# GpSimd's share of the weight splitting: four subtractions of 256 columns in place of one of 1024

## The chip, the core and the metric

The kernel runs on one core of a Trainium2 chip. The metric is the device time of one execution in microseconds, as the median of several executions. The core has a matrix engine (TensorE, written PE in the profile, with its weight loads apart as PEld), VectorE (DVE), ScalarE (ACT), GpSimd (POOL) and SyncE (SP), which here only issues loads and stores. Each engine works through its own list of instructions in order, and semaphores tie the lists together.

## The reference

One decoder layer over 512 tokens of width 1024, all in float32: a norm, one wide projection, three token mixers (dilated window attention, a gated recurrence, block attention), their gated sum, an output projection, and a gated feed-forward block, with a last norm. Cut to its frame:

```python
def hybrid_layer(x, ...):
    h = rms_norm(x, g_mix)
    z = h @ w_in                                   # 1024 x 7936
    qa, ka, va, xb, gb, qc, kc, vc, gates = jnp.split(z, offs, axis=-1)
    ...                                            # A: 12 heads in three dilations
    o_b = rg_lru_branch(xb, gb, conv_w, conv_b, ...)
    o_c = moba_attention(qc, kc, vc, rel_bias[:, A_HEADS:])
    gt = jax.nn.sigmoid(gates).reshape(B, S, 3, D)
    merged = gt[:, :, 0] * (o_a @ p_a) + gt[:, :, 1] * (o_b @ p_b) + gt[:, :, 2] * (o_c @ p_c)
    x = x + merged @ w_out
    u = rms_norm(x, g_ffn) @ w_gu
    gate, up = jnp.split(u, 2, axis=-1)
    return x + (jax.nn.silu(gate) * up) @ w_down
```

## The kernel before

**Split products.** The kernel keeps float32 accuracy by writing each operand as a high half (rounded to the type `F32R`) and a low half (what the rounding left out), and by forming three products for each pair: high by high, high by low, low by high (`mm3`, lines 195 to 198). Nearly all of TensorE's work is these triples, with 512 columns each.

**Weight chunks.** All weights are packed on the host into 149 chunks of 128 x 1024 floats, in the order in which the program uses them (`chunk_plan`). `stage_g` (lines 164 to 182) brings in one chunk in three steps: SyncE issues the load into `wraw` (line 177), ScalarE rounds it into the high half `whi` (line 178), and an engine subtracts, `wlo = wraw - whi` (line 179). That engine is GpSimd for the chunks 7 to 61 and VectorE for the others, by this line:

```python
eng = nc.gpsimd if 6 < i < N_POOL else nc.vector     # N_POOL = 62
```

There are 3 buffers of `wraw` and 4 each of `whi` and `wlo`. `chunk` stages up to two chunks ahead of the one that is handed out. Chunks 7 to 61 belong to the projections of the three mixers and of the gates, up to about 410 us of the run.

**Stages.** The order of the program is: norm statistics and the first projections; values for mixer A and its four head groups j (`la`, `wa`, `wa2`, `ta`, `xa`) woven between projections; mixer C head pairs (`lc`, `wc`, `tc_`, `xcm`); mixer B in four blocks (`b_head`, `b_gate`, `b_tail`, `b_end`); the gated merge; the output projection; the feed-forward block (from about 500 us on) and the down projection with the last norm.

**Places that the text below speaks of.** `ea` with `q_tiles` and `k_tiles` makes the operands of the logits from scaled projections `qt` and `kt` (lines 465, 515, 520). `values_out` (lines 450, 451) copies values out of PSUM. `renorm` (line 922) scales the eight reloaded tiles `xt` by the norm. `class_logits` (lines 572 to 585) multiplies and adds biases; its last step (line 581) is what frees its PSUM bank for the next projection. `wa` (line 590: exponentials on ScalarE) stores its sums through a small DRAM tile `exch`, and `wa2` (lines 721 to 741) reads the partner's sums back, makes a factor in a chain of tiny VectorE steps (lines 724, 726, 727, 732, 735, 737, 739, with one exponential on ScalarE, line 729) and scales the probabilities (line 595). `flip` and `flip_pairs` transpose these on TensorE (lines 604 and 618). `b_tail` and `b_end` (lines 887 to 897) end mixer B: `gb = gb * a` on VectorE (line 896), rounded by ScalarE (line 248).

**What sets the order.** The program is written in one order, and a scheduler in the program builder sets the list of each engine from it, by its own estimate of how long each instruction takes (`schedule_with_timeline_sim=True`, line 1334). So an instruction that is cut into pieces can move others. It also tracks which part of a tile an instruction reads or writes.

Of the kernel before, what the change touches and what calls it, by code (L numbers as in the profile page):

```python
# [131 lines left out]
def layer_kernel(tc, x0p, xT, wts, tab, oneh, msk, idn, gfin, out):  # L132
    nc = tc.nc
# [3 lines left out]
    with (  # L137
# [10 lines left out]
        def uid(s):  # L148
            cnt[0] += 1
            return f"{s}_{cnt[0]}"  # L150

        def slot(dt=F32, s="s"):
            return sp.tile([128, 512], dt, name=uid(s), tag="s")
# [4 lines left out]
        def f32(ap):  # L158
            return ap.bitcast(F32)
# [4 lines left out]
        def stage_g():  # L164

            i = pos[0]
            if i >= len(plan):
                return
            pos[0] += 1
            raw = wp.tile([128, 1024], F32, name=uid("wraw"), tag="wraw", bufs=3)  # L170
            hi = wp.tile([128, 1024], F32R, name=uid("whi"), tag="whi", bufs=4)
            lo = wp.tile([128, 1024], F32R, name=uid("wlo"), tag="wlo", bufs=4)
            eng = nc.gpsimd if 6 < i < N_POOL else nc.vector
            n = FIRST_W if i < 2 else 1024
            for c in range(0, 1024, n):
                cc = slice(c, c + n)
                nc.sync.dma_start(raw[:, cc], wts[i, :, cc])
                nc.scalar.copy(hi[:, cc], raw[:, cc])  # L178
                eng.tensor_sub(lo[:, cc], raw[:, cc], f32(hi[:, cc]))  # L179
                if i < 2:  # L180
                    yield
            ready.append((plan[i][0], hi, lo))

        def stage():
            for _ in stage_g():
                pass
# [78 lines left out]
        xts = []  # L265
        X = []
        parts = [stage_g(), stage_g()]
        for k in range(KT):
            if k == 0:
# [4 lines left out]
            for p in FIRST[k]:  # L274
# [3 lines left out]
            hi = slot(F32R, "xhi")  # L278
            nc.scalar.activation(hi, xt, AF.Copy, scale=g)
            lo = slot(F32R, "xlo")  # L280
            nc.vector.scalar_tensor_tensor(
                lo, in0=xt, scalar=g, in1=f32(hi), op0=ALU.mult, op1=ALU.subtract
# [798 lines left out]
        for m in range(8):  # L1081
# [7 lines left out]
            for b in (0, 2, 1):  # L1089
                ps = bank()  # L1090
                nk = len(O[b])
                for k in range(nk):
                    hi, lo = pc[kk // 8]
                    c = slice((kk % 8) * 128, (kk % 8) * 128 + 128)
# [17 lines left out]
        for m in range(8):  # L1112
# [9 lines left out]
            hi = slot(F32R, "uhi")  # L1122
            nc.scalar.activation(hi, x1, AF.Copy, scale=g)
            lo = slot(F32R, "ulo")
# [70 lines left out]
        for tb in range(4):  # L1195
# [4 lines left out]
            for c0, c1 in cuts:  # L1200
                hf, cc = c0 // 512, slice(c0 % 512, c0 % 512 + c1 - c0)
# [15 lines left out]
                eng = nc.vector if c1 == 1024 and tb == 3 else nc.gpsimd  # L1217
# [9 lines left out]
            for c0, c1 in ((0, 256), (256, 512), (512, 1024)) if tb == 3 else ((0, 512), (512, 1024)):  # L1227
                hf, cc = c0 // 512, slice(c0 % 512, c0 % 512 + c1 - c0)
                y = y2[hf][:, cc]
                nc.vector.tensor_scalar(out=y, in0=y, scalar1=r0, scalar2=t3, op0=ALU.mult, op1=ALU.mult)  # L1230
                eng = nc.sync if c0 != 256 else nc.scalar
# [106 lines left out]
```

## Time and profile before

| | |
|---|---|
| median of 3 executions | 902.32 us (902.29 to 904.23) |
| profiled execution: its own time | 902.25 us |
| its span, first to last instruction | 900.5 us |
| mean granted TensorE clock | 0.991 of full speed |
| TensorE busy | 881.0 us (98%) |
| VectorE busy | 489.2 us (54%) |
| ScalarE busy | 398.8 us (44%) |
| GpSimd busy | 249.6 us (28%), of it 135.2 us in the 55 subtractions of line 179 |

Times in the views are microseconds from the span's start; "mean ns" and the min/median/max of one line are nanoseconds. In a timeline each row gives start, duration, engine, line, operation, tile written from tiles read, shape and count, and in brackets how long the engine had idled before and what ended the idle time. A duration runs from the start of the instruction on its engine to its end, so an instruction that was held up after its start shows a long duration and no idle time. PEclk is the granted clock of TensorE: 1.00 is the upper of its two levels (2.4 GHz), 0.50 the lower (1.2 GHz).

### The profile page before, as it was taken

To read this page: it belongs to the slowest core of one execution; us is meant where nothing else is said; L and a number is where in the kernel's file an instruction comes from. 1 tells how busy PE (TensorE), PEld (TensorE's weight loads), DVE (VectorE), ACT (ScalarE), POOL (GpSimd) and SP (SyncE) were. 2 spreads that over 40 slices of the span, in tenths; PEclk is the share of its full clock that TensorE was granted. 3 is DMA by queue.
4 is the path that set the end of the run, shared out by engine and by line. 5 is a ranking of instruction groups with operands and counts; after the bars stand their busy time and mean duration, and the time that the engine had idled before them with its cause. 6 is when DMAs were issued, how large, how long until landed. Compare 5 with 4: busy or idle time off the path is not lost.

```text
span 900.5 us, 11072 instructions
## 1 busy us (share of the span) xinstructions
PE 881.0 (98%) x4166; PEld 739.8 (82%) x4166; DVE 489.2 (54%) x922; ACT 398.8 (44%) x692; POOL 249.6 (28%) x163
## 2 busy tenths in 40 slices
PE   9998999989999999999999999999999999999996
PEld 7887988868888888878888888888888888888885
DVE  7498957575665566765533536444444444322226
ACT  7375754654666556872222434333223322211213
POOL 2144353444343333346311221111111122100004
PEclk9999999999999999999999999999999999999999
DMA  7254332542322221123222413222322222222202
GB/s 277 86 160 98 98 118 71 114 113 80 110 89 82 94 94 71 71 94 117 94 102 86 140 71 108 95 91 88 109 96 94 94 94 93 97 106 103 93 24 94
DMA packets 40278, 90.27 MB, mean 100 GB/s; under 512 B 13988, under 2 KB 15780, under 8 KB 40224
## 3 DMA queue, kind: packets, MB, share of 16 engines
q1 hardware_dynamic: 34048, 88.26, 29.4%
q10 hardware_dynamic: 5824, 0.98, 0.7%
q8 instruction: 33, 0.54, 0.2%
q0 software_dynamic: 352, 0.33, 0.1%
q14 instruction: 21, 0.17, 0.1%
HBM read 87.34 MB, written 2.20 MB: 99 GB/s over the span
## 4 chain that ended last, share of the span: by engine, by line
PE 82%; DVE 10%; ACT 5%; issue 1%; DMA 1%; SPq 0%; DVEq 0%; ACTq 0%
PE ps L196 22%; PE ps L197 22%; PE ps L198 21%; PE ps L1185 12%; PE ps L655 1%; PE ps L604 1%; DVE xt L922 1%; DVE gb L896 1%; PE ps L551 1%; ACT whi L178 1%; PE ps L550 1%; ACT P L590 1%; DVE P L595 1%; DMA xt<-in_xT 1%; DVE a L891 1%
## 5 line engine op out<-in xcount | busy, mean ns | idle before, releaser
L178 ACT CAST whi<-wraw 128x1024 fp32r<-128x1024 f32 (+1 forms) x149 | 154.5, 1038 | 267.4 <-issue 101.7
L196 PE MATMUL ps<-hi,whi 128*128 128x512 f32 x520 | 206.3, 397 | 1.1 <-ACT hi L248 1.1
L197 PE MATMUL ps<-lo,whi 128*128 128x512 f32 x520 | 203.8, 392 | 0.2 <-DVE lo L249 0.2
L198 PE MATMUL ps<-hi,wlo 128*128 128x512 f32 x520 | 203.6, 392 | 0.0
L179 POOL TENSOR_TENSOR wlo<-wraw,whi 128x1024 fp32r<-128x1024 f32 x55 | 135.2, 2460 | 226.4 <-ACT whi L178 226.0
L179 DVE TENSOR_TENSOR wlo<-wraw,whi 128x1024 fp32r<-128x1024 f32 (+1 forms) x94 | 118.2, 1258 | 113.8 <-ACT whi L178 113.8
L196 PE MATMUL ps<-uhi,whi 128*128 128x512 f32 x352 | 137.9, 392 | 0.0
L198 PE MATMUL ps<-uhi,wlo 128*128 128x512 f32 x352 | 137.1, 389 | 0.0
L197 PE MATMUL ps<-ulo,whi 128*128 128x512 f32 x352 | 136.9, 389 | 0.0
L198 PEld LDWEIGHTS ps<-hi,wlo 128*128 128x128 f32 x520 | 98.2, 189 | 20.7
L196 PEld LDWEIGHTS ps<-hi,whi 128*128 128x128 f32 x520 | 98.4, 189 | 20.4 <-ACT hi L248 1.5
L197 PEld LDWEIGHTS ps<-lo,whi 128*128 128x128 f32 x520 | 98.4, 189 | 19.4 <-DVE lo L249 0.5
L1159 POOL TENSOR_TENSOR av<-sg,uu 128x512 f32<-128x512 f32 x22 | 45.8, 2080 | 198.4 <-DVE sg L1157 198.4
L198 PEld LDWEIGHTS ps<-uhi,wlo 128*128 128x128 f32 x352 | 66.1, 188 | 14.0
L196 PEld LDWEIGHTS ps<-uhi,whi 128*128 128x128 f32 x352 | 66.1, 188 | 13.5
L197 PEld LDWEIGHTS ps<-ulo,whi 128*128 128x128 f32 x352 | 66.1, 188 | 13.4
L1185 PE MATMUL ps<-wlo,hi 128*128 128x512 f32 (+1 forms) x180 | 57.7, 384 | 0.0
L1185 PE MATMUL ps<-whi,lo 128*128 128x512 f32 (+1 forms) x180 | 57.6, 384 | 0.0
L1185 PE MATMUL ps<-whi,hi 128*128 128x512 f32 (+1 forms) x180 | 57.2, 384 | 0.0
L1155 DVE TENSOR_TENSOR uu<-ps,rb 128x512 f32<-128x512 f32 x22 | 15.2, 690 | 64.9 <-PE ps L198 64.9
L196 PE MATMUL ps<-whi,xhi 128*128 128x256 f32 (+1 forms) x128 | 40.7, 322 | 0.3 <-DVE stn L558 0.3
L197 PE MATMUL ps<-wlo,xhi 128*128 128x256 f32 (+1 forms) x128 | 40.9, 319 | 0.0
(232 smaller groups left out, 1223.1 us busy)
## 6 DMA issues: line engine op xcount, KB each, us to landing
wraw<-in_wts SPq DMA_DIRECT2D x145, 512.0 KB, 3.2
xt<-in_xT SPq DMA_DIRECT2D x15, 256.0 KB, 5.5
bias<-relb SPq DMA_DIRECT2D x8, 256.0 KB, 5.9
xr<-in_xT SPq DMA_DIRECT2D x8, 256.0 KB, 2.7
out<-y SPq DMA_DIRECT2D x7, 256.0 KB, 2.1
wraw<-in_wts SPq DMA_DIRECT2D x4, 256.0 KB, 4.8
bias<-relb SPq DMA_DIRECT2D x4, 128.0 KB, 3.8
bias<-relb SPq DMA_DIRECT2D x8, 64.0 KB, 3.9
```

What stands on the lines that cost most here:

```text
L178: nc.scalar.copy(hi[:, cc], raw[:, cc])
L179: eng.tensor_sub(lo[:, cc], raw[:, cc], f32(hi[:, cc]))
L196: nc.tensor.matmul(o, lh, rh, start=start, stop=False)
L197: nc.tensor.matmul(o, lh, rl, start=False, stop=False)
L198: nc.tensor.matmul(o, ll, rh, start=False, stop=stop)
L550: nc.tensor.matmul(bk, qh[:, qc], kk[:, k0 : k0 + nn], start=True, stop=False)
L551: nc.tensor.matmul(bk, ql[:, qc], kk[:, k0 : k0 + nn], start=False, stop=True)
L590: nc.scalar.activation(lay[qb][0], lay[qb][0], AF.Exp, scale=-1.0, bias=negm[:, qb : qb + 1], accum_out=den[:, qb : qb + 1])
L595: nc.vector.tensor_scalar(out=lay[qb][0], in0=lay[qb][0], scalar1=f[:, qb : qb + 1], scalar2=None, op0=ALU.mult)
L1155: nc.vector.tensor_mul(uu, pu, r2)
L1159: nc.gpsimd.tensor_mul(av, sg, uu)
L1185: nc.tensor.matmul((acc[tb][hf] if o is None else o)[:, cc], l[:, t], r[:, hf * 512 + cc.start : hf * 512 + cc.stop], start=((k == 0 or fi ...
```

## The change

Where GpSimd does the subtraction, the chunk's 1024 columns are subtracted in four instructions of 256 columns. VectorE's chunks keep one instruction. Nothing else in the source changes, and the arithmetic is the same.

```diff
                 nc.scalar.copy(hi[:, cc], raw[:, cc])
-                eng.tensor_sub(lo[:, cc], raw[:, cc], f32(hi[:, cc]))
+
+                p = 256 if eng is nc.gpsimd else n
+                for d in range(c, c + n, p):
+                    dd = slice(d, d + p)
+                    eng.tensor_sub(lo[:, dd], raw[:, dd], f32(hi[:, dd]))
```

In the changed file every line behind this one stands four lines further on: its line 590 of before is 594, and so on. The numbers in the tile names (`whi_2079`) also shift.

In GpSimd's list each chunk's subtraction becomes a run of four. Before, around the chunks that are used near 100 us:

```order
L179 TENSOR_TENSOR wlo_975<-wraw_973,whi_974 128x1024
L179 TENSOR_TENSOR wlo_981<-wraw_979,whi_980 128x1024
L179 TENSOR_TENSOR wlo_1163<-wraw_1161,whi_1162 128x1024
L179 TENSOR_TENSOR wlo_1169<-wraw_1167,whi_1168 128x1024
L610 MEMSET ph_1226 128x128
```

After:

```order
L183 TENSOR_TENSOR wlo_996<-wraw_994,whi_995 128x256 x4
L183 TENSOR_TENSOR wlo_1005<-wraw_1003,whi_1004 128x256 x4
L183 TENSOR_TENSOR wlo_1190<-wraw_1188,whi_1189 128x256 x4
L183 TENSOR_TENSOR wlo_1199<-wraw_1197,whi_1198 128x256 x4
L614 MEMSET ph_1259 128x128
```

The order of the chunks among GpSimd's other work stays as it was.

ScalarE's list changes where the last head group of mixer A takes its exponentials (`P` and `dd` are the probabilities and their sums, `z` a gate, `ee` the factor of `wa2`), at 186 to 191 us of the profile. Before:

```order
L590 ACTIVATE P_1943,dd_2030<-P_1943,stp_1868 128x128
L590 ACTIVATE P_1964,dd_2030<-P_1964,stp_1868 128x128
L178 CAST whi_2079<-wraw_2078 128x1024
L905 ACTIVATE z_1903<-ps_1910 128x512
L590 ACTIVATE P_1943,dd_2030<-P_1943,stp_1868 128x128
L590 ACTIVATE P_1964,dd_2030<-P_1964,stp_1868 128x128
L590 ACTIVATE P_1943,dd_2030<-P_1943,stp_1868 128x128
L590 ACTIVATE P_1964,dd_2030<-P_1964,stp_1868 128x128
L729 ACTIVATE ee_1989<-df_1986 128x8
```

After:

```order
L178 CAST whi_2145<-wraw_2144 128x1024
L909 ACTIVATE z_1963<-ps_1973 128x512
L594 ACTIVATE P_2006,dd_2093<-P_2006,stp_1925 128x128
L594 ACTIVATE P_2027,dd_2093<-P_2027,stp_1925 128x128
L594 ACTIVATE P_2006,dd_2093<-P_2006,stp_1925 128x128
L594 ACTIVATE P_2027,dd_2093<-P_2027,stp_1925 128x128
L594 ACTIVATE P_2006,dd_2093<-P_2006,stp_1925 128x128
L594 ACTIVATE P_2027,dd_2093<-P_2027,stp_1925 128x128
L733 ACTIVATE ee_2052<-df_2049 128x8
```

The rounding of a chunk and a gate's activation, which stood in the middle of the eight exponentials, now stand ahead of them.

On TensorE the rows that move near there are these (lines 604 and 618 are transposes of the scaled probabilities, 196 to 198 a gate's projection). Before, at 193 to 199 us:

```order
L604 MATMUL ps_2106<-ident,P_1704 128x128 x3
L196 MATMUL ps_2084<-hi_966,whi_1905 128x512
L197 MATMUL ps_2084<-lo_967,whi_1905 128x512
L198 MATMUL ps_2084<-hi_966,wlo_1906 128x512
L618 MATMUL ps_2119<-ident,P_1727 128x128 x4
L618 MATMUL ps_2136<-ident,P_1748 128x128
L196 MATMUL ps_2157<-hi_931,whi_2046 128x512
L197 MATMUL ps_2157<-lo_932,whi_2046 128x512
L618 MATMUL ps_2136<-ident,P_1748 128x128 x3
L198 MATMUL ps_2157<-hi_931,wlo_2047 128x512
```

After:

```order
L200 MATMUL ps_2153<-hi_987,whi_1965 128x512
L608 MATMUL ps_2160<-ident,P_1757 128x128 x2
L608 MATMUL ps_2160<-ident,P_1758 128x128
L608 MATMUL ps_2175<-ident,P_1758 128x128 x3
L201 MATMUL ps_2153<-lo_988,whi_1965 128x512
L202 MATMUL ps_2153<-hi_987,wlo_1966 128x512
L622 MATMUL ps_2188<-ident,P_1781 128x128 x4
L622 MATMUL ps_2205<-ident,P_1802 128x128
L200 MATMUL ps_2229<-hi_952,whi_2109 128x512
L201 MATMUL ps_2229<-lo_953,whi_2109 128x512
L202 MATMUL ps_2229<-hi_952,wlo_2110 128x512
L622 MATMUL ps_2205<-ident,P_1802 128x128 x3
```

One matmul moves ahead of the transposes of line 604, and one ahead of the last three of line 618; the rest keeps its place. Up to 178 us TensorE's list differs only inside the projection of the values at 50 to 57 us, and VectorE's list up to 220 us not at all. SyncE issues one bias load behind the eight reloads of `xt` (58 us) that it issued ahead of them.

## The prediction

> **What bounds the kernel now.** I read the page's engine shares first, then the busy time by stage, then what TensorE waits for, then the timeline at each wait.
>
> ```profile
> PE 881.0 (98%) x4166; PEld 739.8 (82%) x4166; DVE 489.2 (54%) x922; ACT 398.8 (44%) x692; POOL 249.6 (28%) x163
> ```
>
> TensorE is the bound, so only its idle time and its slow time can be won. By stage (columns: length, PE busy, then the other engines, granted clock, DMA):
>
> ```profile
> 60.00:116.00 56.00, 49.87 (x297) 45.42 (x296) 50.94 (x131) 36.24 (x93) 20.70 (x10) 0.94 0.45 120
> 116.00:190.00 74.00, 74.00 (x376) 62.83 (x376) 44.48 (x134) 43.50 (x107) 33.65 (x22) 1.00 0.42 112
> 190.00:210.00 20.00, 16.50 (x67) 12.73 (x66) 11.57 (x30) 8.72 (x21) 7.63 (x6) 0.83 0.39 92
> 210.00:395.00 185.00, 185.00 (x914) 155.65 (x913) 118.33 (x250) 117.33 (x217) 71.89 (x53) 1.00 0.25 86
> 395.00:410.00 15.00, 13.66 (x59) 10.75 (x59) 8.86 (x8) 8.91 (x11) 10.54 (x5) 1.00 0.31 106
> 410.00:901.00 491.00, 483.25 (x2163) 400.50 (x2161) 212.34 (x275) 147.19 (x194) 91.85 (x53) 1.00 0.27 95
> ```
>
> From 60 to 410 us TensorE idles 6.13, 3.50 and 1.34 us in three stretches and nowhere else. In the first two the clock was also low: 0.06 of 56 us and 0.17 of 20 us are 3.4 us each. All of it is 17.8 us; the 7.75 us behind 410 us lie at the tail, where GpSimd has no chunks. What it waits for:
>
> ```profile
> PE ps L618 <- DVE P L595: 3.9, 3, 2.6
> PE ps L196 <- DVE m L581: 2.9, 1, 2.9
> PE ps L572 <- DVE v L451: 2.1, 2, 1.2
> PE ps L196 <- ACT hi L248: 1.1, 1, 1.1
> ```
>
> No row names GpSimd: TensorE never waits for a low half. It waits for VectorE, and the timeline shows what VectorE waited for. The longest wait, at 75.5 us:
>
> ```profile
> 74.47 2.87 POOL L179 TENSOR_TENSOR wlo<-wraw,whi 128x1024 fp32r<-128x1024 f32 x1 [5.11 <-ACT whi L178]
> 75.05 2.84 DVE L922 SCALAR_TENSOR_TENSOR xt<-xt,prm,rb 128x512 f32<-128x512 f32 x1
> 77.81 0.28 DVE L581 CUSTOM_DVE_ANT_0 P<-ps,P 128x128 f32<-128x128 f32 x1
> 78.46 0.57 PE L196 MATMUL ps<-xhi,whi 128*128 128x512 f32 x1 [2.95 <-DVE m L581]
> ```
>
> The step of line 922 started 0.58 us after GpSimd's subtraction and ended 0.55 us after the subtraction's end (77.34). The two exclude each other: whoever comes second stands until the other's instruction is done. The same at the other places:
>
> ```profile
> 193.23 2.41 POOL L179 TENSOR_TENSOR wlo<-wraw,whi 128x1024 fp32r<-128x1024 f32 x1 [1.65 <-ACT whi L178]
> 193.32 2.34 DVE L724 TENSOR_TENSOR mm<-stp 128x4 f32<-128x4 f32 x1
> 198.05 2.43 POOL L179 TENSOR_TENSOR wlo<-wraw,whi 128x1024 fp32r<-128x1024 f32 x1 [2.12 <-ACT whi L178]
> 197.01 3.75 DVE L595 TENSOR_SCALAR P<-P,ff 128x128 f32<-128x128 f32 x8
> 399.16 3.15 POOL L179 TENSOR_TENSOR wlo<-wraw,whi 128x1024 fp32r<-128x1024 f32 x1 [2.23 <-ACT whi L178]
> 400.16 2.70 DVE L896 TENSOR_TENSOR gb<-gb,a 128x512 f32<-128x512 f32 x1
> 403.58 0.50 PE L196 MATMUL ps<-hi,whi 128*128 128x512 f32 x1 [1.11 <-ACT hi L248]
> ```
>
> A step on 128 x 4 elements took 2.34 us. Behind the long waits the clock falls to its lower level; behind the 1.11 us at 402 us it doesn't:
>
> ```profile
> 80.00:82.00 2.00, 2.00 (x6) 0.50 0.35 4
> 200.00:205.00 5.00, 4.38 (x12) 0.50 0.75 211
> 400.00:405.00 5.00, 3.66 (x15) 1.00 0.30 106
> ```
>
> **The change part by part.** *Price of the pieces.* No 128 x 256 subtraction stands in the trace; the nearest rows are GpSimd's other two-input steps with 256 columns:
>
> ```profile
> L1218 POOL TENSOR_TENSOR y<-x,gf 128x256 f32<-128x256 f32 x1 | 0.7, 749 | 0.0
> L783 POOL TENSOR_TENSOR hp<-hp 64x256 f32<-64x256 f32 x8 | 5.8, 731 | 7.4 <-DVE hp L780 7.1
> L179 POOL TENSOR_TENSOR wlo<-wraw,whi 128x1024 fp32r<-128x1024 f32 x55 | 135.2, 2460 | 226.4 <-ACT whi L178 226.0
> ```
>
> A chunk costs 4 x 0.73 to 0.75 = 2.9 to 3.0 us in place of 2.46, so 55 chunks cost 25 to 30 us more of GpSimd. I cost that at nothing: the last row shows 226.4 us of idle time in front of these subtractions, and a gate's chunk lasts TensorE 24 matmuls at 0.23 us, 5.5 us, so GpSimd keeps up. If that cover were gone, it would be 0.5 us per chunk. TensorE's added waits, now one per piece, cost nothing for the same reason, and the first comes earlier: a matmul that reads the first columns needs one piece.
>
> *Does VectorE get its turn between two pieces?* The nearest rows are two whole chunks back to back (the second row is from the chain of waits):
>
> ```profile
> 66.53 2.83 POOL L179 TENSOR_TENSOR wlo<-wraw,whi 128x1024 fp32r<-128x1024 f32 x1
> 67.04 3.53 DVE xt L922 x2
> ```
>
> The second subtraction followed the first by no gap and took 2.83 us, 0.43 more than alone, because a waiting step of line 922 went in between (the next two of that line start at 67.04). The next step of 922 then stood until the subtraction's end (66.53 + 2.83 = 69.36). So the two take turns, one instruction each. From this follows the price: a contending VectorE step waits 0 to 0.75 us where it waited 0 to 2.4; but where VectorE issues such steps one after another, each one waits for a piece, and four steps pay about what one paid.
>
> *Stretch 60 to 116.* VectorE's contending steps between 40 and 120 us, by form:
>
> ```profile
> L515 DVE TENSOR_TENSOR kk<-kt,kk 64x256 fp32r<-64x256 f32 x16 | 11.9, 741 | 0.3
> L922 DVE SCALAR_TENSOR_TENSOR xt<-xt,prm,rb 128x512 f32<-128x512 f32 x8 | 11.2, 1450 | 0.0
> L922 DVE SCALAR_TENSOR_TENSOR xt<-xt,prm,rb x8: 741/744/2865, 64.9 to 75.1; 128x512 f32<-128x512 f32 x8
> L515 DVE TENSOR_TENSOR kk<-kt,kk x16: 599/610/2660, 48.8 to 97.1; 64x256 fp32r<-64x256 f32 x16
> L520 DVE TENSOR_TENSOR kk<-ps,kk x10: 683/684/694, 133.7 to 304.4; 64x512 fp32r<-64x512 f32 x10
> L520 DVE TENSOR_TENSOR kk<-kt,kk x2: 1472/1756/2041, 46.1 to 93.6; 64x512 fp32r<-64x512 f32 x2
> ```
>
> The last four rows give shortest, median and longest. Undisturbed, a step of 922 takes 0.744 us, so the eight lost 8 x 0.706 = 5.6 us; ahead of them one step of 515 (49 us) lost 2.66 - 0.61 = 2.1 and one of 520 (46 us) 2.04 - 0.68 = 1.4, by its form that reads PSUM and is never held up. After the change these two lose about 0.5 and 0.75, so VectorE reaches line 922 2.3 us earlier. The eight come nearly without a break against eight and then four pieces: seven waits of about 0.7 us, 4.9 in place of 5.6. TensorE's wait for 581 then ends 2.3 + 0.7 = 3.0 us earlier. It does not vanish: TensorE itself comes earlier too (its 2.1 us at line 572 go), so it stalls as long and its clock falls as before. Later in the stretch the four steps of 515 at 95 us, free before, meet the pieces of the chunk ahead: up to 4 x 0.65 = 2.6 us, of which one step of 520 paid 0.8 before. I take -1.1 us there, with 0 and -1.8 as ends.
>
> *Stretch 190 to 210.* Four free steps of 595 last 1.07 us; ScalarE stood idle before its exponentials, and the moved rounding and gate fit in there:
>
> ```profile
> 192.32 1.07 DVE L595 TENSOR_SCALAR P<-P,ff 128x128 f32<-128x128 f32 x4
> 186.52 0.40 ACT L590 ACTIVATE P<-P,stp 128x128 f32<-128x128 f32 x1 [1.30 <-DVE stp L581]
> ```
>
> That brings the chain of `wa2` about 1.0 us forward. Line 724 no longer loses 2.2 us, but 724, 726 and 727 each contend, 3 x 0.65 = 2.0; the eight steps of 595 lost 1.6 us (3.75 against 8 x 0.27) to one subtraction and now meet four pieces, up to 2.6. Sum 1.0 + 0.2 - 1.0 = +0.2 us, between -1 and +6.9 (both waits and the clock's fall gone: 3.5 + 3.4).
>
> *At 400 us.* One long step, 896, behind one subtraction: it waits for one piece at most and ends 1.4 us earlier or more; TensorE's wait and the 0.23 us behind it go: +1.3 us.
>
> *Sum*: 3.0 - 1.1 + 0.2 + 1.3 = 3.4 us, off the profiled execution's own 902.25 us (0.07 below the median shown): **898.8 us**.
>
> The Trainium skill's "SBUF — State Buffer", section "Who interferes with whom", names the mechanism: VectorE steps with two SBUF inputs, or in a two-port mode, and GpSimd share a port pair that the first to issue holds for its whole instruction. The trace agrees (2.34 us for 128 x 4 elements). It also says that the order of issue decides who stands, which is the second rival.
>
> **The rivals.** *A. GpSimd keeps the place between its pieces.* Then VectorE stands for all four, 2.9 to 3.0 us, 0.5 more than now, at each of the eight steps that stand ahead of a TensorE wait (520, 515, three of 922, 724, 595, 896): 902.25 + 8 x 0.5 = 906.3. It decides as soon as contending steps again show over 2.4 us. Against it stands the turn at 67.04; for it, that the second subtraction there had its own load to wait for, while pieces follow with no wait at all. The Trainium skill's "GPSIMD Engine Reference", section "Instruction dispatch", speaks for it: a GpSimd core starts its share of the next instruction when it has finished its share of this one, without waiting for the other cores. No run here shows that.
>
> *B. Taking turns eats the gain.* VectorE's contending steps come in runs (eight of 922, eight of 595, the small steps of `wa2`), and each pays a piece. With the upstream 2.3 us eaten as well (515 comes four in a row) and the 1.8 us end at 95 us, 3.0 - 2.3 - 1.8 + 0.2 + 1.3 = 0.4: 901.9. For it: these runs are what precedes the two largest waits. Against it: single steps paid at 46, 400 and 110 us:
>
> ```profile
> 110.19 1.90 DVE L735 TENSOR_TENSOR ds<-wd 128x4 f32<-128x4 f32 x1
> ```
>
> *C. The waits get short enough for the clock.* If VectorE wins most turns, the eight of 922 lose 2 us rather than 4.9 and both waits fall to about 1 us, which left the clock up at 402 us: 3.4 + 2.9 + 3.4 (the clock in one stretch) = 9.7, so 892.6.
>
> **How the numbers follow.** Forecast 0.45, A 0.12, B 0.30, C 0.13. A measurement of this kernel can tell about 0.3%, 2.7 us, from no change: faster is below 899.6, slower above 905.0. The forecast's own range comes from its ends at 95 us (0 to -1.8) and at 190 us (-1 to +2, where the clock still falls): gains of 1.5 to 6.3, 896.0 to 900.7. Some three quarters of it lie below 899.6: 0.33, C adds 0.13 and B 0.01: faster 0.47. Slower is most of A, 0.10, and 0.03 of B with a new wait: 0.13. The rest, 0.40, is no change. The range reaches over B into A and towards C: 893.5 to 904.5.
>
> **What would show it.** Subtractions: 220 of 0.70 to 0.75 us. VectorE: no step of 922, 724 or 896 over 1.5 us (forecast), over 2.9 us (A), or the sum of 922 still at 11 us with none long (B). TensorE: the wait for 581 ends near 75.4 us, the wait at 402 us is gone, the clock still dips near 80 and 200 us (C: no dip). I am wrong if TensorE gets a wait for GpSimd, or if a wait appears in 116 to 190 or 210 to 395 us.

## The result and the profile after

The changed kernel takes 889.14 us (median of 4 executions, 888.29 to 889.82) where the one before takes 902.91 us in the same comparison (902.29 to 904.23). The ratio is 0.9842, 95% interval 0.9829 to 0.9854. The forecast was 898.8 us, in a range of 893.5 to 904.5: the direction was right, the gain is four times the one forecast, and the time lies below the range.

The profiled execution has a span of 886.6 us, 13.9 us less. Its engine shares and its stages (columns as before: length, busy time of TensorE, its weight loads, VectorE, ScalarE and GpSimd, granted clock, DMA):

```profile
PE 875.2 (99%) x4166; PEld 737.4 (83%) x4166; DVE 472.8 (53%) x922; ACT 399.3 (45%) x692; POOL 283.9 (32%) x328
60.00:116.00 56.00, 53.01 (x331) 49.24 (x331) 46.63 (x133) 38.61 (x98) 31.10 (x38) 0.97 0.56 129
190.00:210.00 20.00, 20.00 (x99) 16.85 (x99) 11.52 (x28) 10.25 (x19) 11.60 (x16) 1.00 0.41 133
395.00:410.00 15.00, 15.00 (x68) 12.43 (x67) 9.21 (x11) 4.31 (x5) 9.51 (x7) 1.00 0.28 105
```

GpSimd is busy 34 us longer, and TensorE has no idle time and no low clock left at 190 us, none at 400 us, and half of each at 60 to 116 us. What TensorE still waits for is four rows:

```profile
PE ps L200 <- DVE m L585: 2.2, 1, 2.2
PE wu L264 <- DVE ser L1019: 1.1, 1, 1.1
PE ps L576 <- DVE v L455: 0.4, 1, 0.4
PE ps L200 <- DVE stn L562: 0.3, 1, 0.3
```

The same steps before and after place the 13.9 us. The transposes of line 618 (now 622) run from 113.5 to 232.6 us before, the last copies of the merged tiles (line 248, now 252) start at 487.5 us:

```profile
L618 PE MATMUL ps<-ident,P x32: 270/273/474, 113.5 to 232.6; 128*128 128x128 f32 x32
L248 ACT ACTIVATE hi<-mgs x8: 632/632/634, 411.8 to 487.5; 128x512 fp32r<-128x512 f32 x8
```

```profile
L622 PE MATMUL ps<-ident,P x32: 270/272/329, 108.2 to 220.6; 128*128 128x128 f32 x32
L252 ACT ACTIVATE hi<-mgs x8: 631/632/633, 397.0 to 473.6; 128x512 fp32r<-128x512 f32 x8
```

By 113.5 us the kernel is 5.3 us ahead, by 232.6 us 12.0 us, by 487.5 us 13.9 us. So the stretches gave **5.3, 6.7 and 1.9 us**. The forecast had 1.9 (3.0 - 1.1), 0.2 and 1.3.

**At 62 to 75 us**, GpSimd and VectorE in the changed kernel:

```profile
62.14 7.93 POOL L183 TENSOR_TENSOR wlo<-wraw,whi 128x256 fp32r<-128x256 f32 x8 [8.14 <-ACT whi L178]
63.27 3.14 DVE L926 SCALAR_TENSOR_TENSOR xt<-xt,prm,rb 128x512 f32<-128x512 f32 x3 [0.32 <-DMA xt<-in_xT]
67.57 1.89 DVE L926 SCALAR_TENSOR_TENSOR xt<-xt,prm,rb 128x512 f32<-128x512 f32 x2
70.05 3.01 DVE L926 SCALAR_TENSOR_TENSOR xt<-xt,prm,rb 128x512 f32<-128x512 f32 x3
73.63 0.47 PE L200 MATMUL ps<-xhi,whi 128*128 128x512 f32 x1 [2.20 <-DVE m L585]
```

The eight steps of line 926 (922 before) begin 1.7 us earlier (63.27 us for 64.94) and take 3.14 + 1.89 + 3.01 = 8.0 us against 11.2. The two make 4.8 us, and TensorE's wait ends 4.8 us earlier, at 73.63 us (78.46 before).

**At 190 us**, the chain that ends mixer A's last head group (5.3 us of shift is already in these times):

```profile
185.44 2.96 POOL L183 TENSOR_TENSOR wlo<-wraw,whi 128x256 fp32r<-128x256 f32 x4 [2.43 <-ACT whi L178]
185.60 0.72 DVE L728 TENSOR_TENSOR mm<-stp 128x4 f32<-128x4 f32 x1
186.36 0.66 DVE L730 TENSOR_TENSOR df<-mm,stp 128x4 f32<-128x4 f32 x1
188.86 1.66 DVE L599 TENSOR_SCALAR P<-P,ff 128x128 f32<-128x128 f32 x8
189.26 0.92 PEld L622 LDWEIGHTS ps<-ident,P 128*128 128x128 f32 x5 [0.24 <-PE ps L201]
```

The tiny step that took 2.34 us takes 0.72, the eight scalings 1.66 us in place of 3.75, and the transposes of line 622 wait for TensorE's own matmul (0.24 us) and no longer for the scalings. Further up the same chain VectorE forms the low half of `oa` (line 246, now 250). Before, this step met a whole subtraction that began at 180.04 us; all later steps of the chain stand behind it. Before and after:

```profile
180.65 2.36 DVE L246 TENSOR_TENSOR lo<-oa,hi 128x512 fp32r<-128x512 f32 x1 [5.69 <-ACT hi L245]
```

```profile
175.63 0.69 DVE L250 TENSOR_TENSOR lo<-oa,hi 128x512 fp32r<-128x512 f32 x1 [6.14 <-ACT hi L249]
```

### The profile page after: what moved, and what is told of

The parts are those of the page before. It is cut to its first block, busy times and chain, and to the rows that moved or that the text cites. A ratio compares the mean times of both kernels' runs of the same rounds, so it can differ in the third digit from the quotient of the medians.

```text
span 886.6 us, 11269 instructions
## 1 busy us (share of the span) xinstructions
PE 875.2 (99%) x4166; PEld 737.4 (83%) x4166; DVE 472.8 (53%) x922; ACT 399.3 (45%) x692; POOL 283.9 (32%) x328
## 4 chain that ended last, share of the span: by engine, by line
PE 88%; DVE 4%; issue 3%; POOL 2%; DMA 2%; ACT 1%; DVEq 0%; POOLq 0%; ACTq 0%
PE ps L200 23%; PE ps L201 23%; PE ps L202 23%; PE ps L1189 12%; POOL wlo L183 2%; DMA wraw<-in_wts 2%; PE ps L659 2%; PE ps L608 1%; PE ps L555 1%; PE ps L554 1%; DVE y L1234 1%; DVE lo L250 0%; PE ps L622 0%; PE ps L780 0%; ACT junk L1220 0%
## 5 line engine op out<-in xcount | busy, mean ns | idle before, releaser
L183 POOL TENSOR_TENSOR wlo<-wraw,whi 128x256 fp32r<-128x256 f32 x220 | 169.6, 803 | 181.1 <-ACT whi L178 181.0
L1222 POOL TENSOR_TENSOR y<-x,gf 128x512 f32<-128x512 f32 (+1 forms) x8 | 9.7, 1229 | 108.3 <-DVE x L1212 107.9
```

What stands on the lines that cost most here:

```text
L183: eng.tensor_sub(lo[:, dd], raw[:, dd], f32(hi[:, dd]))
L1222: eng.tensor_mul(y2[hf][:, cc], x, gf[hf][:, cc])
```

## The experiments

Theory T: VectorE stood behind a whole subtraction, and what pays is that it now stands behind a quarter. Rival O: the scheduler's new order pays. Beside them stood two models of the price of one turn: W, the prediction's (a contending step stands for up to a whole piece), and S (only the streaming of columns excludes, the fixed parts of both instructions overlap). The kernel before took 903.4 to 903.8 us in the comparisons below, about 1 us more than the expectations reckon with, so each gain is taken from the ratio.

**e1: the new order with the old length.**

```diff
-                p = 256 if eng is nc.gpsimd else n
-                for d in range(c, c + n, p):
-                    dd = slice(d, d + p)
+                cut = [0, 1000, 1008, 1016, 1024] if eng is nc.gpsimd else [c, c + n]
+                for d, e in zip(cut, cut[1:]):
+                    dd = slice(d, e)
```

> Four subtractions per chunk as in the changed kernel, but of 1000, 8, 8 and 8 columns, so that one of them is nearly as long as the old one; the lists of VectorE, ScalarE and SyncE are the changed kernel's row for row, TensorE's differ from it by one matmul. Theory T (the gain is that VectorE stands for a quarter chunk at most): the long steps come back, a step of line 926 of over 2 us, 728 at 2.3 us near 190 us, TensorE waits at 585 for 2.5 us or more, and the time is 899 to 902 us, since only the moved order at 190 us helps (some 1 us). Rival O (the gain is the scheduler's new order): 888 to 891 us, as the changed kernel.

902.38 us, ratio 0.9981 (0.9970 to 0.9991): 1.7 us of gain. The long steps are back:

```profile
L926 DVE SCALAR_TENSOR_TENSOR xt<-xt,prm,rb x8: 739/742/2593, 66.3 to 77.1; 128x512 f32<-128x512 f32 x8
L728 DVE TENSOR_TENSOR mm<-stp x4: 150/157/2316, 103.8 to 222.0; 128x4 f32<-128x4 f32 x4
PE ps L622 <- DVE P L599: 4.0, 2, 2.0
```

Rival O falls: with the changed kernel's lists, and one long piece in each chunk, nearly all of the gain is gone. The time is a little above T's, and the wait for 585 was 2.0 us and not 2.5 or more. At 190 us the new order alone did not shorten TensorE's waits for the scalings: they sum to 4.0 us there, 3.5 before.

**e2, e3, e4: the pieces for a part of the chunks.** Each adds a condition on the chunk's index `i` to the line that sets `p`:

```diff
-                p = 256 if eng is nc.gpsimd else n
+                p = 256 if eng is nc.gpsimd and i < 20 else n         # e2
+                p = 256 if eng is nc.gpsimd and 19 < i < 45 else n    # e3
+                p = 256 if eng is nc.gpsimd and 44 < i else n         # e4
```

> Pieces of 256 only for the chunks 7 to 19 (up to about 125 us); later chunks in one piece. ScalarE's list is that of before, row for row. Theory T: the gain of the stretch up to 116 us alone, 5.3 us by the two traces: 897 us; the two waits and the low clock at 190 to 205 us are back as before. Rival O: nearly nothing, 901 to 902 us, because the moved exponentials are not in it.

> Pieces of 256 only for the chunks 20 to 44 (about 125 to 300 us). ScalarE's and VectorE's lists are those of the changed kernel, SyncE's differs in one load. Theory T: the gain of the stretch at 190 us alone, 6.7 us by the two traces: 895.5 us; the wait at 581 near 75 us stays at 2.9 us. Rival O: the whole gain, 889 us, if the order alone makes it.

> Pieces of 256 only from chunk 45 on (behind about 300 us). TensorE's, ScalarE's and SyncE's lists are those of before, row for row. Theory T: the gain of the last stretch alone, 1.9 us by the two traces: 900.4 us, with no wait of TensorE at 402 us. Rival O: no change, 902.3 us. If the three parts add up, e2, e3 and e4 together save 13.9 us.

| | median | ratio (95%) | gain by the ratio |
|---|---|---|---|
| e2, chunks 7 to 19 | 898.70 us | 0.9937 (0.9918 to 0.9956) | 5.7 us |
| e3, chunks 20 to 44 | 897.14 us | 0.9934 (0.9919 to 0.9949) | 6.0 us |
| e4, chunks 45 to 61 | 902.39 us | 0.9983 (0.9974 to 0.9993) | 1.5 us |

The sum is 13.2 us, and the whole change has 14.3 us (1.58% of 903): within intervals of about 1 to 2 us on each gain the stretches add up, each by about what the traces gave it. e4's 902.39 us looks like rival O's 902.3, but its ratio is below 1 (a gain of 0.6 to 2.3 us). It is the plainest test, since its lists on TensorE, ScalarE and SyncE are those of before; its trace has no wait of TensorE at 400 us.

**e5 and e6: pieces of 512 and of 128.** The same line, with `p = 512` and `p = 128`.

> Two pieces of 512 columns per chunk. Model W (the prediction's: a contending VectorE step stands for up to a whole piece): a piece takes about 1.29 us, a step of line 926 at worst 0.74 + 1.29 = 2.03 us. Model S (only the streaming of columns excludes, 0.55 us per 256 columns and 0.53 us for a step of 926; the fixed 0.19 us of each hides under the other): a step and a piece follow each other every 0.53 + 1.11 = 1.64 us. Both give a gain between none and the changed kernel's: 893 to 898 us, with waits of TensorE near 75 and 190 us that are shorter than before.

> Eight pieces of 128 columns. A piece alone should take 0.19 + 0.28 = 0.46 us. Model W: the contending steps of line 926 take up to 0.74 + 0.46 = 1.2 us, as in the changed kernel, so no further gain: 888 to 890 us. Model S: a step and a piece follow each other every 0.53 + 0.28 = 0.81 us, a contending step of 926 shows about 0.9 to 1.0 us, the eight sum to 6.6 to 7 us in place of 8.04, and TensorE's wait for 585 falls from 2.2 to about 1.2 us; if the clock then stays up, 885 to 887.5 us, if not 887.5 to 888.5.

512: 895.69 us, ratio 0.9910 (0.9896 to 0.9925). 128: 890.25 us, ratio 0.9853 (0.9839 to 0.9868). The steps of 926 (shortest, median, longest in ns), of e5, of the changed kernel and of e6:

```profile
L926 DVE SCALAR_TENSOR_TENSOR xt<-xt,prm,rb x8: 735/1378/1773, 63.8 to 74.5; 128x512 f32<-128x512 f32 x8
```

```profile
L926 DVE SCALAR_TENSOR_TENSOR xt<-xt,prm,rb x8: 737/1214/1228, 63.3 to 71.9; 128x512 f32<-128x512 f32 x8
```

```profile
L926 DVE SCALAR_TENSOR_TENSOR xt<-xt,prm,rb x8: 740/940/951, 66.8 to 74.3; 128x512 f32<-128x512 f32 x8
```

A contending step takes longer than one alone by 2.12 us behind 1024 columns (2.865 - 0.744, the row of before), 1.03 behind 512, 0.48 behind 256 and 0.20 behind 128. That is a line: about 2.14 ns per column of the piece, less 0.07 us. Model S foretold these steps (0.9 to 1.0 us at 128); W's worst cases, 2.03 and 1.2 us, did not come (the longest are 1.77 and 0.95). So a turn at 256 columns costs 0.48 us, and the 0.74 us that a piece lasts is no measure of it.

Over all 128 gives no more than 256, as W had it and against S, which had 885 to 888.5 us. In e6's trace TensorE's wait for 585 fell to 0.3 us, but VectorE reached the steps of 926 late, and TensorE waited ahead of them:

```profile
66.79 2.64 DVE L926 SCALAR_TENSOR_TENSOR xt<-xt,prm,rb 128x512 f32<-128x512 f32 x3 [3.06 <-DMA xt<-in_xT]
70.13 0.47 PE L576 MATMUL ps<-kk,qq 128*128 128x256 f32 x2 [1.66 <-DVE stn L562]
```

The loads of `xt` stand in SyncE's list behind bias loads, which read a table that GpSimd itself stores (line 399), and that store is in GpSimd's list behind the pieces. In e6, and in the changed kernel run again (e14 below, whose execution starts alike):

```profile
46.32 10.06 POOL L183 TENSOR_TENSOR wlo<-wraw,whi 128x128 fp32r<-128x128 f32 x16 [13.37 <-ACT whi L178]
56.32 1.51 POOL L399 DMA_DIRECT2D relb<-rows  x3
60.33 0.81 SPq L406 DMA_DIRECT2D bias<-relb  x2
```

```profile
54.01 1.52 POOL L399 DMA_DIRECT2D relb<-rows  x3
57.89 1.76 SPq L406 DMA_DIRECT2D bias<-relb  x4
```

Two chunks in sixteen pieces take 10 us, the store goes 2.3 us later, the bias loads 2.4 us, and the steps of 926 begin at 66.8 and not at 64.7 us. The cost of the pieces, which the prediction called hidden, comes out there. It is not the whole reason: e13 below has pieces of 128 with loads that are not late, and gains nothing either.

**e7: GpSimd without subtractions**, as the ceiling.

```diff
+                if eng is nc.gpsimd:
+                    lo = hi
+                else:
+                    eng.tensor_sub(lo[:, cc], raw[:, cc], f32(hi[:, cc]))
```

> GpSimd subtracts nothing: for the chunks 7 to 61 the product with the low half is formed with the high half again, so the low halves of these weights are left out of the result, with the same number of matmuls. It shows what is left to win behind the pieces. Theory T: every step of line 926 at 0.74 us, the eight at 5.9 us, 2.1 us less than with pieces, so the wait for 585 is nearly gone with the clock's fall behind it: 884 to 886 us. If the wait stays at 2 us, it is VectorE's own work and not GpSimd's that makes it: 888 to 889 us.

883.35 us, ratio 0.9772 (0.9756 to 0.9789), a little faster than forecast. In the stretch that the change left unfinished TensorE is never idle and never slow:

```profile
60.00:116.00 56.00, 56.00 (x362) 52.98 (x361) 41.45 (x136) 41.51 (x104) 0.41 (x2) 1.00 0.62 152
```

Between 60 and 410 us no wait of TensorE is left, and the run is about 6 us below the changed kernel: so much is still to be had there. Not all of it need be the holding of VectorE, since ScalarE's roundings stand at other places in this version's list and the buffers come free without GpSimd.

**e8 and e9 to e11: moving the eight steps of 926.** In e8 the call `reload()`, which issues the loads of `xt`, moves five lines down, behind `wa(d0)`; in e9 to e11 six lines up, ahead of the four calls of `ea`, with pieces of 256, 128 and 1024.

> The changed kernel with the eight reloads of xt issued behind the exponentials of the first head group (one call moved five lines down), so that the scheduler puts the eight steps of line 926 behind the steps of line 585 and not ahead of them. Theory T: TensorE's wait for 585 near 73 us goes, 2.2 us and the 1.7 us of the lower clock: 885 to 886 us. Rival V: the steps only move to where the projection at 95 us waits for the split tiles, and a wait of about the same length stands there: 888 to 890 us.

> The changed kernel with the eight reloads of xt issued earlier (one call moved six lines up): SyncE's list has them ahead of the loads of the chunks of 48 us, VectorE's list has the eight steps of line 926 at 40 to 46 us, behind the first use of rb and mostly ahead of GpSimd's subtraction of 45 us. Theory K (VectorE's own chain of work sets the wait for 585): the eight take 8 x 0.66 = 5.3 us in place of about 7.5, and VectorE's idle 1.7 us ahead of line 926 falls away, so 585 ends 2 to 3.7 us earlier and the time is 885 to 887.5 us, although TensorE now waits longer for line 455 near 60 us. Rival V: the stall only moves to line 455, with the clock's fall behind it: 888.5 to 891 us.

> Pieces of 128 columns with the early reloads, so that the loads of xt are no longer late as with pieces of 128 alone (there VectorE stood 3.06 us for them at 66.8 us). Model S: the steps that still contend pay 0.20 us and not 0.48: 0 to 1.5 us below the kernel with pieces of 256 and early reloads. Rival: GpSimd's added 0.9 us a chunk now stands in the way of the loads of the next chunks (three buffers): 0 to 2 us above it.

> One subtraction of 1024 columns as before, with the early reloads alone. If the eight steps of line 926 were what the first stretch lost to GpSimd, this gets the stretch's gain without pieces: 5 us, 897 us, with the waits at 190 and 400 us as before. If the other steps (515, 520, 465) pay as much, the gain is 2 us or less: 900 to 902 us.

e8, e9 and e11 missed every expectation. e8: 904.92 us, ratio 1.0013 (1.0000 to 1.0025). The wait for 585 is gone, as T said, but VectorE stood 11.92 us for the loads with the urgent steps queued behind, and TensorE stood longer than ever:

```profile
88.13 2.12 DVE L926 SCALAR_TENSOR_TENSOR xt<-xt,prm,rb 128x512 f32<-128x512 f32 x3 [11.92 <-DMA xt<-in_xT]
99.53 0.55 PE L554 MATMUL ps<-kk,qh 128*128 128x256 f32 x1 [9.48 <-DVE kk L524]
```

e9: 896.11 us, ratio 0.9916 (0.9898 to 0.9935); e10: 894.93 us, 0.9903 (0.9881 to 0.9924); e11: 905.64 us, 1.0027 (1.0016 to 1.0037). Here the steps of 926 stand ahead of line 479, which reads projections out of PSUM and so frees banks that TensorE needs, a consumer that the expectation had not looked at:

```profile
PE ps L200 <- DVE kt L479: 3.8, 1, 3.8
```

(that row is e9's). e10 is 1.2 us below e9, as model S had it, but the two intervals overlap widely. The runs don't separate the theories that they were meant for; they show that neither of the two other places tried for these eight steps is better than the one they have.

**e12: pieces at 190 us with the old order.** `28 < i < 33` in the same line; the lists of TensorE, VectorE, ScalarE and SyncE are those of before.

> Pieces of 256 only for the chunks 29 to 32, those subtracted at 180 to 200 us; the lists of TensorE, VectorE, ScalarE and SyncE are those of before, row for row. With e1 (new order, long subtraction: 1.5 us) and e3 (both: 6.5 us) it tells how much of the gain at 190 us is the pieces' own. If the pieces do it alone: 895.5 to 897 us. If they need the moved exponentials (595 starts some 1 us too late without them): TensorE keeps a wait of about 1 us for 595, the clock may fall, and the time is 898 to 900.5 us.

900.98 us, ratio 0.9970 (0.9959 to 0.9982): 2.7 us.

```profile
198.63 2.62 DVE L599 TENSOR_SCALAR P<-P,ff 128x128 f32<-128x128 f32 x8
199.07 1.08 PE L622 MATMUL ps<-ident,P 128*128 128x128 f32 x5 [1.52 <-DVE P L599]
199.67 2.88 POOL L183 TENSOR_TENSOR wlo<-wraw,whi 128x256 fp32r<-128x256 f32 x4 [1.93 <-ACT whi L178]
```

These pieces leave a wait of 1.52 us and a low clock behind it (0.91 over 190 to 210 us). The four chunks are subtracted at 190 to 209 us; the subtraction that began at 181.52 us is still whole in e12, and the step of line 250 stood behind it as before:

```profile
182.12 2.36 DVE L250 TENSOR_TENSOR lo<-oa,hi 128x512 fp32r<-128x512 f32 x1 [5.70 <-ACT hi L249]
```

In e3 that step takes 0.69 us, and between 190 and 210 us TensorE has no wait and a clock of 1.00. So e12 lacks both the new order and a piece that matters, and doesn't tell what either is worth. Nor do the times show that pieces and order give more together than apart: e12's 2.7 us (1.6 to 3.7) and e1's 1.7 us (0.9 to 2.7) against e3's 6.0 us (4.6 to 7.3).

**e13 and e14: does a cheaper turn reach the end?** e13 is the changed kernel with `p = 128` for the chunks 10 to 12, those that meet line 926; e14 is the changed kernel again.

> The changed kernel with pieces of 128 columns for the chunks 10 to 12 alone, those that meet the eight steps of line 926; all lists but SyncE's (one pair of loads) are the changed kernel's. Model S: a contending step of 926 takes 0.94 us and not 1.22, the eight 6.7 us and not 8.0, so TensorE's wait for 585 is 0.9 to 1.3 us shorter; the time is 1 to 3 us below the changed kernel in this call (the larger if the clock stays up). Rival: the chain of VectorE sets the pace up to 100 us, but what is won is lost again at a later wait there: 0 to 0.5 us.

> The changed kernel itself, for comparison on the same chip: 888 to 890 us.

e13: 892.27 us, ratio 0.9874 (0.9861 to 0.9888). e14: 889.73 us, 0.9854 (0.9836 to 0.9872). The intervals overlap; e13 is not faster, and its median is 2.5 us above e14's, which neither S (1 to 3 us below) nor the rival (0 to 0.5) had. Its own trace shows S's step and then the loss:

```profile
73.80 0.47 PE L200 MATMUL ps<-xhi,whi 128*128 128x512 f32 x1 [0.90 <-DVE m L585]
83.53 1.05 ACT L178 CAST whi<-wraw 128x1024 fp32r<-128x1024 f32 x1 [2.19 <-POOL wlo L183]
85.15 1.94 DVE L469 TENSOR_TENSOR ql<-qt,qh 64x512 fp32r<-64x512 f32 x2 [2.66 <-ACT qh L498]
101.50 0.46 PE L200 MATMUL ps<-whi,xhi 128*128 128x256 f32 x1 [2.50 <-DVE stn L562]
```

The wait for 585 ended 1.34 us earlier than in e14 (75.14), and the wait at 101 us ended 0.23 us later (e14: 101.27 us, a wait of 1.54). In between ScalarE stood 2.19 us ahead of a rounding, with the rounding of `qh` behind it, and VectorE stood for that. The view names GpSimd's subtraction as what ended it; why it is waited for here and not in e14, whose lists differ by one exchange of loads on SyncE, stays open. What is won at 74 us is lost by 101 us. The loads of `xt` were in time here (the steps of 926 begin at 64.55 us).

Apart from e7, which leaves out the low halves of 55 chunks, no version ran faster than the changed kernel.

## Why the prediction was wrong, step by step

Two steps of the sum failed. The price of one turn was taken as a whole piece, 0.7 us, where it is 0.48: at the eight steps of line 922 that forecast a gain of 0.7 us, and 3.2 came. And at 190 us the sum had 0.2 us where the chain up to the scalings won 4.9, so that TensorE's wait and the clock's fall there both went.

- **The bound and the mechanism: right.** TensorE lost its time in the stretches named, waiting for VectorE, and VectorE was standing behind GpSimd's instruction. e1 (long piece, new order) and e7 (no subtraction) show both sides of it.
- **The price of the pieces: right.** A piece takes 0.716 us at the shortest, 0.740 as the median, for the 0.73 to 0.75 taken from other steps. TensorE got no wait for GpSimd, and no new wait appeared in 116 to 190 or 210 to 395 us. GpSimd's added time showed as some 0.3 us ahead of the step of line 246 (below), and with pieces of 128 (e6) through its own store and the loads that wait for it.
- **"VectorE reaches line 922 2.3 us earlier": nearly right.** The first of the last steps ahead of it (line 451, now 455) begins at 59.76 us and not at 61.84: 2.1 us. The steps of 922 themselves begin 1.7 us earlier, since VectorE then waits 0.32 us for the loads of `xt`.
- **"Seven waits of about 0.7 us, 4.9 in place of 5.6": wrong, and the first cause.** This is the term that was mis-sized: 0.7 us was the whole piece, and a turn costs 0.48 us (e5, e6 and the line through four sizes). Of the eight steps five paid a turn of about 0.48 us: 1207 to 1228 ns, three others 737, 740 and 848. Together they lost 2.5 us (8 x 0.310, the mean of the row below less 0.744) where they had lost 5.6. The gain at this place was 3.2 us and not 0.7, and the wait ended 4.8 us earlier and not 3.0. The Trainium skill's "SBUF — State Buffer", section "Who interferes with whom", has the holder keep the port pair for its whole instruction; by that a step behind a piece of 0.74 us could lose 0.74, and the rows show 0.48. The measurement decides: a part of the two instructions, some 0.26 us here, runs at the same time. Which part that is inside the engines, no run shows.

```profile
L926 DVE SCALAR_TENSOR_TENSOR xt<-xt,prm,rb 128x512 f32<-128x512 f32 x8 | 8.0, 1054 | 0.3 <-DMA xt<-in_xT 0.3
```

- **"It stalls as long and its clock falls as before": half wrong.** The clock fell twice in this stretch, at 65 to 68 and at 79 to 82 us. The first fall, behind the 0.9 and 1.2 us at line 572, is gone with those waits; the text had them going but not the fall. The second fall stayed in this execution, behind a wait of 2.20 us where it was 2.95; in e14's it did not come behind 2.18 us. Over 56 us the clock is 0.97 in place of 0.94, 1.7 us. That is no gain on top of the 4.8 us: TensorE's wait ends when VectorE is done, whatever TensorE's clock was before.
- **"-1.1 at 95 us": wrong.** The four steps of 515 lost 0.4 us and the step of 520 won as much (1.09 us for 1.47). TensorE's wait near 100 us ends 4.8 us earlier too (100.14 us for 104.90), so nothing was lost on the way. Most of the half microsecond up to 5.3 is the wait for 595 at 113 us (0.4 us), which is gone.
- **190 us, "1.0 + 0.2 - 1.0": wrong, and the larger miss.** TensorE had come 5.4 us forward up to 177 us; the eight scalings of line 595 end 10.2 us earlier (190.52 us for 200.76). So the chain that leads to them won 4.9 us by itself, and the sum had 0.2. Two of its terms hold: ScalarE's moved work gave 0.8 (1.0 forecast), and the steps from 724 to 739 gave 0.4 (0.2 forecast; 724 to 727 won 1.1, but 732 and 735, free before, lost 0.7 to pieces). The eight steps of 595 were to lose another 1.0; they won 2.1, because the chain arrived early enough for most of them to be done when the next subtraction began (1.52 us behind their start; 1.04 before). In e12 they took 2.62 us for four pieces, still 1.1 us less than before. And a term is missing: the step of line 246 at 180.65 us, which the prediction did not count among those held up, won 1.7 us, of which some 0.3 went to GpSimd's own steps ahead of it, now later by its pieces. With the wait gone the clock's fall went too. The end of +6.9 us, named as a bound, is what came (6.7); the range had only +2 there, on the ground that the clock would still fall.
- **400 us: right** in kind, +1.3 forecast, 1.5 us by e4's ratio, 1.9 by the trace.
- **The rivals.** A (no turn between pieces) never showed: no step of 922, 724 or 896 lasts over 1.23 us. B (turns eat the gain) rested on the overpriced turn. C was the nearest, and its 2 us for the eight steps is close to the 2.5 that they lost, but its waits of about 1 us did not come: the one near 75 us was 2.2 us, the one at 200 us vanished. The chance of 0.13 for it came from pricing a turn by the duration of an instruction. The trace of before could have told more: the step of 75.05 us ended 0.55 us behind the subtraction, although it takes 0.74 alone, so part of it had run under the subtraction.

## What to carry to other kernels

Where VectorE steps with two SBUF inputs feed TensorE, price a long GpSimd instruction beside them by its columns: for the float32 subtractions here some 2.1 ns each. Cutting them in four cut the longest loss of a step by more than three quarters for a quarter more GpSimd time. Price a turn from observed steps against two lengths, not from the duration of the instruction. Follow the chain ahead of a stall upwards, past the steps next to it: here the step of line 246, 16 us ahead of the scalings, was worth 1.7 us. And where a stall carries a fall of the clock, give the case that it vanishes a place in the range. Finer pieces are no better by themselves: at 128 columns the slower engine showed up in what is queued behind its pieces, here its own store and the loads that wait for it.

## What the runs showed of the hardware that was not expected

- Exclusion between GpSimd and VectorE is not of whole instructions: a contending step of 512 columns pays 2.14 ns per column of the other's piece less 0.07 us, over pieces of 128, 256, 512 and 1024 columns. The pieces pay too: eight in a row beside steps of 926 took 7.93 us, 0.99 each, against 0.74 alone.
- Similar waits have dissimilar consequences for the clock. Behind the wait of 2.20 us at 71 to 73.6 us the changed kernel fell to the lower level (1.2 GHz; 0.50 from 75 to 78 us). In e2 a wait of 2.19 us at the same instruction had no fall behind it (clock 1.00 from 75 to 100 us), and the fall came behind a later wait of 1.96 us at 101.7 us. In e14, the changed kernel again, waits of 2.18 and 1.54 us at the same two places had no fall behind them (1.00 from 60 to 116 us).
- The clock can dip without any wait of TensorE: between 30 and 40 us it was 0.83 in the profiled execution of e14 and 1.00 in that of the same kernel shown above, some 1.7 us, with TensorE busy throughout. Differences of that size between two single executions say nothing of a change.

```profile
30.00:40.00 10.00, 10.00 (x64) 9.95 (x64) 3.00 (x16) 1.19 (x2) 2.47 (x4) 0.83 0.15 52
```

```profile
30.00:40.00 10.00, 10.00 (x73) 9.52 (x73) 3.01 (x16) 1.62 (x3) 2.41 (x4) 1.00 0.15 52
```

The first row is e14's, the second the changed kernel's of the result.
